# A three-block transformer kernel: the mixer's fourth query block moved ahead of the gate products, and bias rows spread from HBM to HBM

## The chip, the cores and the metric

The kernel runs on one core of a Trainium2 chip. A core has a matrix engine (TensorE, PE in the profile, with its weight loads as PEld), a vector engine (VectorE, DVE), an activation engine (ScalarE, ACT), a general-purpose engine (GpSimd, POOL) and SyncE (SP), which here only issues transfers. Each engine works through its own list of instructions in order and waits on semaphores for the others. Transfers run on 16 DMA engines. The metric is the device time of one execution in microseconds (us).

## The reference

The input x has 512 tokens of 1024 features, and all arithmetic is in float32. Two layers of a first kind are followed by one layer of a second kind:

```
for l in range(2):
    x = x + 0.5 * swiglu_ffn(x, ...)          # 1024 -> 2816 -> 1024
    h = rms_norm(x, mix_norm[l])
    x = x + hybrid_mixer(h, ...)
    x = x + 0.5 * swiglu_ffn(x, ...)
x = second_block(x, ...)                      # dilated attention + convolution, then an ffn
```

The hybrid mixer projects h with w_in and runs three attentions: a stick-breaking one (o_a), one over compressed, selected and window keys (o_b, "NSA", 8 heads), and one over indexed top keys (o_c, "DSA", 4 heads). Then it merges them with gates:

```
g_a, g_b, g_c = split(sigmoid(h @ w_gate), 3)
merged = g_a * (o_a @ w_br_a) + g_b * (o_b @ w_br_b) + g_c * (o_c @ w_br_c)
return merged @ w_out
```

The second block's attention adds a bias that depends on the distance of query and key: 8 rows (heads) of 384 numbers for each of three groups, each a table product of a 32 x 8 table with a 32 x 384 selection matrix plus a mask.

## The kernel before

**Numbers and weights.** A float32 product is made of three fast products: weights and activations are each split into a high and a low part (`split`, `w_prep`), and `mm3` (lines 172 to 174) issues high x high, high x low and low x high. Activations are kept with features on the partitions, so most products are 128 x 128 weights against 512 tokens. The weights come as one stream of 550 units of 128 x 1024 numbers (512 KB). A unit is loaded by SP into one of 3 staging buffers (`w_dma`, line 133), split by an ACT copy (line 141) and a DVE subtraction (line 142) into a ring of 5 slots, 3 units ahead of the products (`LOOK`), and used up by 24 matmuls.

**The first ffn.** `gen_ffn` makes 22 column groups; `up(cs)` takes 16 `mm3` for a group, and the first call takes groups 0 and 1 together and then makes the row norm (`stats_a`, `bcast`: DVE line 231, PE line 232), which the evacuation of every group needs. After `up` of group 2 in the very first ffn, `bias_rows` is called once: for each of three groups a small matmul (line 1015), a DVE addition into 8 rows of 384 numbers on partitions 0 to 7 (line 1018), and a POOL transfer (line 1019) that writes each row 128 times to the HBM buffer `dr_b` (3 x 8 x 128 x 384 numbers). `dr_b` is read in the second block only, on line 1172.

**The mixer.** There are two streams. The main stream, `gen_mix`, issues the projections, then 24 gate products (`tunit("w_gate", ...)`, evacuated on line 522 into the buffers at `M_IQ` and stored by POOL on line 523), then loads the first third of the gates again (line 530), and then forms the products with w_br_a (evacuated on line 538). All of these use the PSUM banks 0 and 1. The side stream, `gen_side`, does the attentions. `drive` interleaves them in the order in which instructions are written: it runs the side stream until it yields the name of a flag, and then steps the main stream until that flag is set. The order that results is only a priority: a planner that works with modelled times puts ready instructions of lower priority into the gaps. On the chip each engine's order is then fixed.

The NSA part, `gen_nsa`, has four query blocks b = 0 to 3 with n = 128 (b + 1) keys. A block has 8 calls of `attn_pair` (lines 760 to 803), each for two heads u: scores (PE line 777) into a bank of the first ring, addition of the mask with its maximum (DVE line 779), exponential (ACT line 781), scaling (DVE line 787), transposition (PE line 793) into a bank of the second ring, copy (ACT line 798), product with the values (PE line 801) into bank 7. A block opens with a matmul on line 898. The preparation of the next block (`prep`) is written into the middle of a block. The DSA part, `gen_dsa`, has four blocks of two such calls. `self.rings` names the two rings of banks, `self.p_ring` and `self.t_ring` the buffers for probabilities and their transposes. For b < 3 the rings are (2, 3, 4) and (5, 6). For block 3 it says:

```
if b == 3:
    yield "gates"
    self.rings = ((2, 3, 4), (5, 6, 0, 1))
...
self.p_ring = (p, p, p + [M_NQ], p + [M_NQ, M_IQ])[b][:4]
```

With n = 512, `p` has two buffers. The rings set for block 3 stay in force for the DSA part.

After both streams `gen_merge` forms the products with w_br_b and w_br_c over all 512 tokens, taking banks from a ring of all eight, adds them on DVE and POOL (lines 983 and 984), and multiplies with w_out.

Of the kernel before, what the change touches and what calls it, by code (L numbers as in the profile page):

```python
# [9 lines left out]
F32 = mybir.dt.float32  # L10
# [41 lines left out]
M_IQ = M  # L52
# [4 lines left out]
M_NQ = M_SV + 1024  # L57
# [52 lines left out]
class Build:  # L110
# [133 lines left out]
    def gen_ffn(self, wgu, wdn, l, done, halves=None):  # L244
        nc = self.nc
        Y = A_Y
        gs = [self.f(Y + 1536 + 512 * i, 512) for i in range(2)]
        tt = [self.f(Y + 2560 + 512 * i, 512) for i in range(2)]
        rb = self.f(A_RB, 512)
        ring = tuple(range(8))  # L250

        def fs(c):
            o = R_O + (c % FSLOTS) * 1024
            return self.r(o, 512), self.r(o + 512, 512)

        def gkey(c, up, k):
            return (wgu, l, np.arange(128 * k, 128 * k + 128), np.arange(128) + 128 * c + up * DFF)

        def evac(c, pg, pu):
            i = c % 2  # L260
            nc.vector.tensor_tensor(gs[i], pg, rb, op=ALU.mult)  # L261
            nc.scalar.activation(gs[i], gs[i], AF.Silu)
            nc.vector.tensor_tensor(gs[i], pu, gs[i], op=ALU.mult)  # L263
            hi, lo = fs(c)
            self.split(hi, lo, gs[i])

        def up(cs):
            ps = {(c, up): self.bank(ring) for c in cs for up in (0, 1)}
            order = [(c, up, k) for c in cs for up in (0, 1) for k in range(8)]
            if len(cs) == 2:  # L270
                order.sort(key=lambda e: e[2])
            for c, up, k in order:
                self.mm3(ps[c, up], self.w(gkey(c, up, k)), self.h(k), k == 0, k == 7)
                yield
            if len(cs) == 2:
                pst = self.bank(ring)
                self.bcast(self.stats_a((self.acc,), pst), tt_flat, pst, rb)
            for c in cs:
                evac(c, ps[c, 0], ps[c, 1])
            if cs[0] == 2 and self.first:  # L280
                self.first = False
                self.bias_rows()

        tt_flat = self.f(Y + 2560, 512)

        def down(grp, cs):
            nk = len(cs)
            if grp == 0:
                order = [(m, j) for m in range(8) for j in range(nk)]
            else:  # L290
                order = [(m, j) for m in range(2) for j in range(nk - 1)] + [(m, nk - 1) for m in range(2)]
                order += [(m, j) for m in range(2, 6 if halves else 8) for j in range(nk)]
            ps = {}
            for m, j in order:
                if j == 0:
                    ps[m] = self.bank(ring)
                key = (wdn, l, np.arange(128) + 128 * cs[j], np.arange(128) + 128 * m)
                self.mm3(ps[m], self.w(key), fs(cs[j]), j == 0, j == nk - 1)
                yield
                if j == nk - 1:  # L300
                    done(grp, m, ps[m], tt[m % 2], rb)
            if grp == 0 or not halves:
                return

            tl = {}
            for i in range(2):
                sl = slice(256 * i, 256 * i + 256)
                for m in (6, 7):
                    ps = self.bank(ring)[:, sl]
                    for j in range(nk):  # L310
                        if i == 0:
                            tl[m, j] = self.w((wdn, l, np.arange(128) + 128 * cs[j], np.arange(128) + 128 * m))
                        self.mm3(ps, tl[m, j], [a[:, sl] for a in fs(cs[j])], j == 0, j == nk - 1)
                        yield
                    done(grp, m, ps, tt[m % 2][:, sl], rb, sl)
                halves(i)

        c0 = list(range(11))
        c1 = list(range(11, 22))
        for cs in [(0, 1)] + [(c,) for c in range(2, 13)]:  # L320
            yield from up(cs)
        yield from down(0, c0)
        for c in c1[2:]:
            yield from up((c,))
        yield from down(1, c1)
# [516 lines left out]
    def gen_nsa(self, l):  # L842
        nc = self.nc
# [41 lines left out]
        nxt = prep(0)  # L885
        for b in range(4):
            q2, pts = nxt
            n = 128 * (b + 1)
            first = [None, None]
            if b == 3:  # L890
                yield "gates"
                self.rings = ((2, 3, 4), (5, 6, 0, 1))
            p = [M_P + 2 * n * i for i in range(1024 // n)]
            t = [o + 2 * n * i for i in range(512 // n) for o in (M_PT, M_SV)]
            self.p_ring = (p, p, p + [M_NQ], p + [M_NQ, M_IQ])[b][:4]
            self.t_ring = (t, t, t, t + [M_NQ + 1024])[b][:4]
            for g in range(2):
                first[g] = mm(ob[64 * g:64 * g + 64], lhsT=vc[:, 64 * g:64 * g + 64], rhs=pts, start=True, stop=True,
                              skip_group_check=True)
            for s in range(2):  # L900
                k = [[self.r(R_QK + 2048 * hl + 512 * (2 * s + g), 512) for hl in range(2)] for g in range(2)]
                for hh in range(4):
                    self.attn_pair([q2[:, 128 * (4 * g + hh):128 * (4 * g + hh) + 128] for g in range(2)], k,
                                   self.f(A_C + C_CM, 512)[:, 512 - n:512], n,
                                   gt[:, b, :, 1 + s].rearrange("p (g h) -> p h g", g=2)[:, hh],
                                   [V[:, :, s, g, :] for g in range(2)], ob[:, 128 * hh:128 * hh + 128], first)
                    self.bg(2)
                    if s == 1 and hh == 1:
                        nxt = prep(b + 1) if b < 3 else self.d_prep(0)
            o = self.r(R_O, 8192).rearrange("p (l c t) -> p l c t", l=2, c=8)[:, :, 2:6, 128 * b:128 * b + 128]  # L910
            self.split(o[:, 0], o[:, 1], ob.rearrange("p (c t) -> p c t", c=4))
# [27 lines left out]
    def gen_side(self, l):  # L939
        yield from self.gen_idx(l)  # L940
        yield from self.gen_cmp(l)
        yield "sb"
        self.sb_pair(0)
        yield "k"
        self.k_prep()
        self.k_tpose(0)
        yield "nq"
        self.q_prep(M_NQ, 8, 80, self.f(M_IQ + 1024, 128))
        self.sb_pair(1)
        self.k_tpose(1)  # L950
        yield "dq"
        self.q_prep(M_DQ, 4, 80 + 256, self.f(A_SM + 256, 64))
        self.rings = ((2, 3, 4), (5, 6))
        nxt = yield from self.gen_nsa(l)
        self.gen_dsa(l, nxt)


# [47 lines left out]
    def bias_rows(self):  # L1005

        nc = self.nc
        o = A_Y + 3584
        cb = self.f(o, 2304)[0:32]
        nc.scalar.dma_start(cb, self.ap["cb"])  # L1010
        tab = self.f(o + 2304, 24)[0:32]
        nc.scalar.dma_start(tab, self.ap["par"][2][0:32, 296:320])
        for g in range(3):
            ps = self.bank(tuple(range(8)))
            nc.tensor.matmul(ps[0:8, 0:384], lhsT=tab[:, 8 * g:8 * g + 8], rhs=cb[:, 384 * g:384 * g + 384],
                             start=True, stop=True)
            t = self.f(o + 2328 + 384 * g, 384)[0:8]
            nc.vector.tensor_tensor(t, ps[0:8, 0:384], cb[0:8, 1152 + 384 * g:1536 + 384 * g], op=ALU.add)
            nc.gpsimd.dma_start(self.dr_b[g], t[:, None, :].to_broadcast([8, 128, 384]))

    def gen_mix2(self):
        nc = self.nc
# [402 lines left out]
    def run(self, upto=99, start=0):  # L1425
        tc, nc, ap = self.tc, self.nc, self.ap
        with tc.tile_pool(name="sb", bufs=1) as sb, tc.tile_pool(name="hp", bufs=1) as self.hp, \
# [9 lines left out]
            self.sqt = [self.f(A_Y + 512 + 512 * i, 512) for i in range(2)]  # L1437
            self.dr_x = dr.tile([128, 4096], F32, name="dr_x")
            self.dr_b = dr.tile([3, 8, 128, 384], F32, name="dr_b")
            self.dr_c = dr.tile([8, 128, 512], F32, name="dr_c")  # L1440
            self.dr_s = dr.tile([512, 12], F32, name="dr_s")
            self.m2 = {}
# [17 lines left out]
            for l in range(2 if start == 0 else 0):  # L1460
                g = par[:, 24 * l:24 * l + 24]
                nxt = par[:, 24 * l + 24:24 * l + 32]
# [122 lines left out]
```

## Time and profile before

| what | value |
|---|---|
| time, median of 3 runs | 3531.94 us (3525.71 to 3532.26) |
| the profiled execution: its time | 3525.48 us |
| the profiled execution: its span, first to last instruction | 3523.7 us |
| mean granted clock of TensorE, as a share of full speed | 0.985 |
| PE busy | 3423.5 us (97%), 16884 records |
| DVE busy | 1998.7 us (57%) |
| ACT busy | 1316.1 us (37%) |
| POOL busy | 320.0 us (9%) |
| DMA traffic | 357.05 MB, mean 101 GB/s |

The busy time of PE is modelled from pipelined matmuls, so two stretches with the same busy share can hold different amounts of work; the number of matmul records in a stretch tells more. A matmul on plain float32 operands leaves two records. Where a line of the trace has "idle ... <-", what follows is the instruction that ended the wait. Times within the execution count from the start of the span.

### The profile page before, as it was taken

How to read it: one execution, taken by the hardware profiler on the slowest of the kernel's cores; microseconds unless marked ns; L12 is line 12 of the kernel's file. 1: busy time of each engine (PE TensorE's matmuls, PEld its weight loads, DVE VectorE, ACT ScalarE, POOL GpSimd, SP SyncE). 2: the span in 40 equal slices, each digit the busy share in tenths (PEclk: the TensorE clock that was granted, in tenths of full speed). 3: DMA queues.
4: the chain of work that ended last, by engine and by line, in shares of the span. 5: the costliest groups of instructions: out<-in, count | busy, mean ns of one | idle time of the engine just before them, and what ended most of it. 6: DMA issues, size and time to landing. Idle time of an engine off the chain costs nothing.

```text
span 3523.7 us, 43236 instructions
## 1 busy us (share of the span) xinstructions
PE 3423.5 (97%) x16884; PEld 2793.6 (79%) x16884; DVE 1998.7 (57%) x3733; ACT 1316.1 (37%) x2234; POOL 320.0 (9%) x355
## 2 busy tenths in 40 slices
PE   6899999999999999999999999999999999999997
PEld 5688888776888888888887768888877777878886
DVE  4344488566544444344886666443488998554344
ACT  3222354356332233223544464322344443443232
POOL 2000100010300010001000104000111112220002
PEclk8999999999999999999999999999999999999998
DMA  6722322331322222223322314223333224522221
GB/s 149 116 99 96 120 91 87 108 115 54 132 96 96 96 96 96 96 100 116 96 89 98 112 42 149 95 97 100 108 105 92 83 79 141 183 80 98 97 96 54
DMA packets 100814, 357.05 MB, mean 101 GB/s; under 512 B 14168, under 2 KB 16984, under 8 KB 99808
## 3 DMA queue, kind: packets, MB, share of 16 engines
q1 hardware_dynamic: 81504, 290.49, 24.6%
q0 software_dynamic: 18144, 61.76, 6.9%
q8 instruction: 132, 2.16, 0.3%
q10 hardware_dynamic: 960, 2.04, 0.2%
q14 instruction: 74, 0.61, 0.1%
HBM read 320.05 MB, written 32.08 MB: 100 GB/s over the span
## 4 chain that ended last, share of the span: by engine, by line
PE 91%; DMA 3%; DVE 3%; ACT 1%; issue 1%; POOL 0%; DVEq 0%; ACTq 0%; POOLq 0%
PE pb L172 27%; PE pb L173 27%; PE pb L174 27%; DMA af<-wst 2%; PE pb L801 2%; PE pb L793 1%; PE pb L777 1%; PE pb L1193 1%; PE pb L595 1%; PE pb L737 1%; PE pb L1290 1%; PE pb L1266 1%; PE pb L756 0%; DVE af L1351 0%; DVE ar L142 0%
## 5 line engine op out<-in xcount | busy, mean ns | idle before, releaser
L141 ACT ACTIVATE ar<-af 128x1024 fp32r<-128x1024 f32 x550 | 582.7, 1060 | 1517.5 <-PE pb L173 968.2
L172 PE MATMUL pb<-h,ar 128*128 128x512 f32 x2848 | 1114.2, 394 | 33.9 <-ACT ar L141 15.1
L174 PE MATMUL pb<-h,ar 128*128 128x512 f32 x2848 | 1120.1, 393 | 0.1
L173 PE MATMUL pb<-h,ar 128*128 128x512 f32 x2848 | 1119.4, 393 | 0.0
L142 DVE TENSOR_TENSOR ar<-af,ar 128x1024 fp32r<-128x1024 f32 x550 | 687.7, 1251 | 447.6 <-ACT ar L141 446.1
L172 PEld LDWEIGHTS pb<-h,ar 128*128 128x128 f32 x2848 | 538.0, 189 | 151.1 <-ACT h L239 16.2
L174 PEld LDWEIGHTS pb<-h,ar 128*128 128x128 f32 x2848 | 537.7, 189 | 114.6 <-issue 3.2
L173 PEld LDWEIGHTS pb<-h,ar 128*128 128x128 f32 x2848 | 537.9, 189 | 113.6 <-issue 3.2
L173 PE MATMUL pb<-ar 128*128 128x512 f32 (+1 forms) x1254 | 483.2, 386 | 1.2 <-DVE ar L183 1.2
L174 PE MATMUL pb<-ar 128*128 128x512 f32 (+1 forms) x1254 | 482.8, 386 | 0.0
L172 PE MATMUL pb<-ar 128*128 128x512 f32 (+1 forms) x1254 | 481.8, 386 | 0.6 <-DVE af L779 0.5
L172 PEld LDWEIGHTS pb<-ar 128*128 128x128 f32 x1254 | 235.6, 188 | 49.4 <-DVE af L779 1.2
L200 POOL TENSOR_TENSOR af<-af 128x512 f32<-128x512 f32 (+1 forms) x76 | 109.7, 1444 | 1816.5 <-ACT af L198 1805.5
L173 PEld LDWEIGHTS pb<-ar 128*128 128x128 f32 x1254 | 235.6, 188 | 49.0 <-DVE ar L183 2.4
L174 PEld LDWEIGHTS pb<-ar 128*128 128x128 f32 x1254 | 235.6, 188 | 47.1
L263 DVE TENSOR_TENSOR af<-pb,af 128x512 f32<-128x512 f32 x110 | 75.6, 690 | 299.0 <-PE pb L174 297.9
L261 DVE TENSOR_TENSOR af<-pb,af 128x512 f32<-128x512 f32 x110 | 75.5, 691 | 247.0 <-PE pb L174 231.9
L1132 DVE SCALAR_TENSOR_TENSOR af<-af 128x512 f32<-128x512 f32 x240 | 179.4, 748 | 3.6
L172 PE MATMUL pb<-ar,h 128*128 128x256 f32 (+1 forms) x448 | 133.4, 298 | 0.0
L173 PE MATMUL pb<-ar,h 128*128 128x256 f32 (+1 forms) x448 | 132.4, 296 | 0.0
L174 PE MATMUL pb<-ar,h 128*128 128x256 f32 (+1 forms) x448 | 132.0, 295 | 0.0
L180 DVE TENSOR_TENSOR ar<-af,ar 128x512 fp32r<-128x512 f32 (+4 forms) x178 | 114.3, 649 | 16.2 <-ACT ar L179 15.6
(236 smaller groups left out, 3185.3 us busy)
## 6 DMA issues: line engine op xcount, KB each, us to landing
af<-wst SPq DMA_DIRECT2D x550, 512.0 KB, 3.3
dr_g<-af POOLq DMA_DIRECT2D x64, 256.0 KB, 2.3
af<-dr_g POOLq DMA_DIRECT2D x24, 512.0 KB, 4.6
dr_x<-af POOLq DMA_DIRECT2D x3, 2048.0 KB, 7.5
af<-dr_x POOLq DMA_DIRECT2D x3, 2048.0 KB, 8.7
dr_b<-af POOLq DMA_DIRECT2D x3, 1536.0 KB, 63.3
h<-dr_g POOLq DMA_DIRECT2D x16, 256.0 KB, 5.5
af<-x POOLq DMA_DIRECT2D x8, 256.0 KB, 12.3
```

The lines of the kernel that those rows point to most:

```text
L141: self.nc.scalar.activation(self.r(o, UNIT), st, AF.Copy)
L142: self.nc.vector.tensor_tensor(self.r(o + UNIT, UNIT), st, self.r(o, UNIT), op=ALU.subtract)
L172: mm(out, lhsT=w[0], rhs=a[0], start=start, stop=False, skip_group_check=True)
L173: mm(out, lhsT=w[0], rhs=a[1], start=False, stop=False, skip_group_check=True)
L174: mm(out, lhsT=w[1], rhs=a[0], start=False, stop=stop, skip_group_check=True)
L180: self.nc.vector.tensor_tensor(lo, src, hi, op=ALU.subtract)
L200: nc.gpsimd.tensor_tensor(acc, acc, t, op=ALU.add)
L261: nc.vector.tensor_tensor(gs[i], pg, rb, op=ALU.mult)
L263: nc.vector.tensor_tensor(gs[i], pu, gs[i], op=ALU.mult)
L595: self.nc.tensor.transpose(ps[:, 128 * i:128 * i + 128], t[:, 128 * i:128 * i + 128], self.f(A_C + C_ID, 128))
L801: first[u] = self.behind(first[u], mm(out[64 * u:64 * u + 64], lhsT=v[u][:, j, :], rhs=pts[u][:, 128 * j:128 * j + 128], start=first[u] is ...
L1132: nc.vector.scalar_tensor_tensor(a, u[:, j:j + 512], w[:, j:j + 1], a, op0=ALU.mult, op1=ALU.add)
```

## The change

Three edits are made.

1. The NSA part no longer yields "gates" ahead of block 3, so block 3 and the DSA part are written, and so ranked, ahead of the gate products. As these hold the banks 0 and 1 and the buffers at `M_IQ`, block 3 and the DSA part keep the rings (2, 3, 4) and (5, 6), and the fourth probability buffer is dropped.
2. `bias_rows` is called after `up` of group 8 instead of group 2.
3. In `bias_rows`, the 8 rows go first to a small HBM buffer `dr_r`, and the 128-fold spreading reads from that buffer: a transfer from HBM to HBM.

```diff
-            if cs[0] == 2 and self.first:
+            if cs[0] == 8 and self.first:
                 self.first = False
                 self.bias_rows()
...
-            if b == 3:
-                yield "gates"
-                self.rings = ((2, 3, 4), (5, 6, 0, 1))
             p = [M_P + 2 * n * i for i in range(1024 // n)]
             t = [o + 2 * n * i for i in range(512 // n) for o in (M_PT, M_SV)]
-            self.p_ring = (p, p, p + [M_NQ], p + [M_NQ, M_IQ])[b][:4]
+            self.p_ring = (p, p, p + [M_NQ], p + [M_NQ])[b][:4]
...
-        nxt = yield from self.gen_nsa(l)
+        nxt = self.gen_nsa(l)
...
-            nc.gpsimd.dma_start(self.dr_b[g], t[:, None, :].to_broadcast([8, 128, 384]))
+            nc.gpsimd.dma_start(self.dr_r[g], t)
+            nc.gpsimd.dma_start(self.dr_b[g], self.dr_r[g][:, None, :].to_broadcast([8, 128, 384]))
...
+            self.dr_r = dr.tile([3, 8, 384], F32, name="dr_r")
```

## Rows read from the trace of the kernel before

**Rows 1.** The page: busy us (share of the span) and records of each engine.
```profile
PE 3423.5 (97%) x16884; PEld 2793.6 (79%) x16884; DVE 1998.7 (57%) x3733; ACT 1316.1 (37%) x2234; POOL 320.0 (9%) x355
```

**Rows 2.** The chain that ended last, in order of time: start us, us, what.
```profile
29.38 27.73 DMA af<-wst
...
87.50 47.47 DMA af<-wst
```

**Rows 3.** Windows of the start: stretch, us, busy us (records), PEclk, DMA share, GB/s.
```profile
40.00:70.00 30.00, 11.40 (x40) 8.28 (x39) 8.76 (x22) 6.54 (x7) 0.00 (x0) 0.66 0.45 106
110.00:150.00 40.00, 24.87 (x85) 18.52 (x84) 12.64 (x16) 10.55 (x14) 0.00 (x0) 0.79 0.89 138
40.00:50.00 10.00, 3.95 (x18) 2.94 (x16) 0.00 (x0) 0.00 (x0) 0.00 (x0) 0.82 0.49 76
110.00:120.00 10.00, 2.81 (x13) 1.99 (x11) 0.00 (x0) 0.00 (x0) 0.00 (x0) 0.91 0.99 93
220.00:260.00 40.00, 40.00 (x178) 33.15 (x177) 16.04 (x19) 8.49 (x8) 0.00 (x0) 1.00 0.29 96
```

**Rows 4.** POOL in order of time, 15 to 150 us: the three spreading transfers.
```profile
22.33 1.11 POOL L1019 DMA_DIRECT2D dr_b<-af  x1
...
74.27 1.09 POOL L1019 DMA_DIRECT2D dr_b<-af  x1 [47.80 <-DVE af L1018]
77.06 1.05 POOL L1019 DMA_DIRECT2D dr_b<-af  x1 [1.70 <-DVE af L1018]
```

**Rows 5.** DMA issues, 0 to 60 us: issues, KB each, us to landing.
```profile
dr_b<-af POOLq DMA_DIRECT2D x1, 1536.0 KB, 35.6
```

**Rows 6.** DMA issues of the whole page: issues, KB each, median us to landing.
```profile
af<-wst SPq DMA_DIRECT2D x550, 512.0 KB, 3.3
...
dr_x<-af POOLq DMA_DIRECT2D x3, 2048.0 KB, 7.5
...
dr_b<-af POOLq DMA_DIRECT2D x3, 1536.0 KB, 63.3
```

**Rows 7.** POOL's DMA queue, 30 to 57 us: packets, MB, share of 16 engines.
```profile
q0 software_dynamic: 280, 1.27, 43.8%
```

**Rows 8.** The same queue and the weight loads issued, 87 to 100 us.
```profile
q0 software_dynamic: 148, 0.68, 96.6%
...
af<-wst SPq DMA_DIRECT2D x2, 512.0 KB, 48.7
```

**Rows 9.** Windows of the two mixers, columns as in group 3.
```profile
800.00:870.00 70.00, 63.04 (x473) 45.84 (x473) 43.78 (x151) 44.92 (x111) 1.64 (x3) 1.00 0.05 15
...
2050.00:2120.00 70.00, 64.08 (x463) 46.70 (x463) 43.49 (x149) 44.45 (x110) 4.19 (x5) 0.93 0.08 24
```

**Rows 10.** DVE in order of time, first mixer: last gate product, last w_br_a product.
```profile
770.09 0.69 DVE L522 TENSOR_TENSOR af<-pb,af 128x512 f32<-128x512 f32 x1
...
791.98 0.69 DVE L538 SCALAR_TENSOR_TENSOR h<-h,pb 128x512 f32<-128x512 f32 x1
```

**Rows 11.** PE in order of time, first mixer: block 3's first scores.
```profile
800.65 1.17 PE L777 MATMUL pb<-ar 128*128 128x512 f32 x4
```

**Rows 12.** The same two moments in the second mixer, DVE and PE.
```profile
2042.61 0.69 DVE L538 SCALAR_TENSOR_TENSOR h<-h,pb 128x512 f32<-128x512 f32 x1 [0.69 <-PE pb L174]
...
2047.18 1.18 PE L777 MATMUL pb<-ar 128*128 128x512 f32 x4
```

**Rows 13.** Groups by line and shape, 800 to 870 us: busy us, mean ns.
```profile
L793 PE MATMUL pb<-af 128*128 128x128 f32 x116 | 17.5, 281 | 2.1 <-DVE af L787 1.1 <-DVE af L875 1.1
L781 ACT ACTIVATE af<-af 128x512 f32<-128x512 f32 x20 | 14.4, 719 | 4.9 <-DVE af L779 4.9
...
L798 ACT ACTIVATE af<-pb 128x512 f32<-128x512 f32 x22 | 12.6, 597 | 4.7 <-PE pb L793 4.7
...
L781 ACT ACTIVATION_READ_ACCUMULATOR af<-af 128x1 f32 x33 | 6.3, 190 | 0.0
```

**Rows 14.** Waits of PE, 800 to 870 us: us in total, times, longest.
```profile
PE pb L801 <- ACT af L798: 1.3, 3, 0.6
```

## The prediction

> **What bounds the kernel now.** I read the page first. PE is busy for 97% of the span [rows 1], so the work is bound by PE's own matmuls, and an edit that adds or removes none can only give back the stretches in which PE stands still or runs at its lower clock. The next view is the chain of waits in order of time. Outside PE it has two long pieces, both waits for a weight load, of 27.7 and 47.5 us [rows 2], where a load takes 3.3 us as a rule [rows 6]. So I looked at windows of the first 260 us. In steady work (220 to 260 us) PE leaves 178 records in 40 us, 4.45 per us [rows 3]. From 40 to 70 us there are 40 records, which is 40 / 4.45 = 9.0 us of work in 30; from 110 to 150 there are 85, which is 19.1 us of work in 40. The losses are 21.0 and 20.9 us, 41.9 together. [...]
>
> What the loads wait behind is seen in the DMA views. Just before each long load POOL issues the spreading transfers of the bias rows: one at 22.3 us, two at 74.3 and 77.1 [rows 4]. The first lands after 35.6 us [rows 5], the other two after 63.3 each [rows 6], where 63.3 is the median of the three and the first is the smaller. One alone keeps POOL's queue busy on 43.8% of the DMA engines' time, near half of them, and moves 1.27 MB in 27 us, 47 GB/s; two together take 96.6% and move 0.68 MB in 13 us, 52 GB/s [rows 7, 8]. Twice the engines move no more bytes. The two weight loads issued beside the pair take a median of 48.7 us [rows 8].
>
> Last I looked at the mixers, where the first edit acts. The end of the attention, 70 us in each mixer, is the one part where PE is not full: 63.0 and 64.1 us busy of 70 [rows 9].
>
> **The change part by part: the spreading transfer.** Its source moves from 8 partitions of SBUF to HBM; bytes, row length (384 numbers, 1536 bytes) and destination stay. What limits it now is common to one and to two transfers: not the number of engines, since the second set adds nothing, but the 8 source partitions or the writing into `dr_b`. HBM takes writes much faster from 128 partitions: 2048 KB in 7.5 us [rows 6]. So I take the source partitions as the limit, and the edit removes it. No row shows a transfer from HBM to HBM, so its cost is bounded from both sides. Fast end: 7.5 x 1536 / 2048 = 5.6 us on all engines, 11.3 us on half of them; of three transfers two share a half, 22.5 us for all. Slow end: no faster than now, 3 x 1.573 MB at the 49.7 GB/s of the pair (3.146 MB in 63.3 us) = 95 us. I take a value near the fast end, since the `dr_x` row is the nearest in what it does to HBM.
>
> [...]
>
> What a slow transfer costs depends on the weights in hand. The load issued at 87.5 us was late, and PE ran on until it had used 2.81 us of the window from 110, to 112.8: cover of 25.3 us [rows 2, 3]. At the first stall it was 29.4 to 43.95, only 14.6 us, the ring not having filled. The later place (after group 8 instead of 2) therefore matters too. A column group is 48 matmuls, at 4.45 per us 10.8 us, so with PE starting near 10 us group 8 ends near 107, and the three transfers are issued there, within some 10 us, when the ring is full. At the fast end a load waits 22.5 us at most, inside the cover, and the loss is nothing. Then both losses go: 41.9 us. I keep 3 us back for the ramp of the start and for loads that arrive late without stopping PE, and book -39.
>
> The added transfer to `dr_r` is three issues, which POOL must each see landed before the spreading issue. Behind it on POOL's queue stands nothing until the end of this ffn, hundreds of us later (POOL's view has no instruction after the third issue up to 150 us, [rows 4]), and SP's queue is not passed. `dr_b` is read far behind, in the second block. This costs nothing; without that cover it would be three short landings. The three small matmuls and additions only move.
>
> **The mixer.** Taking out the wait reorders the writing, so I asked what block 3 waits for now. In the first mixer the last gate product is evacuated at 770.1 us and the last w_br_a product at 792.0 [rows 10], and block 3's first scores start at 800.65 [rows 11]; in the second they are 2042.6 and 2047.2 [rows 12]. So block 3 starts 8.7 and 4.6 us after the last product of the main stream, when block 2 has got that far: the blocks before it, which stand ahead of the gates already, take so long that the gates are used up as filler first. The flag holds up nothing that was ready, and I book 0 gain.
>
> What remains of this edit is what it takes away: two of four banks for the transposed probabilities, and one of four probability buffers. A pair of heads in block 3 has two transpositions of four matmuls. A bank's turn is transposition, wait, copy (597 ns), and the copies share ACT with the exponentials (719 ns and 190 ns each) [rows 13]. Over 800 to 870 us ACT is 44.9 us busy and PE 63.0 [rows 9], so a bank has usually been copied when its turn comes, and PE's waits for a copy are 1.3 us now [rows 14]. Bounds: nothing, and one exponential with its read-out (0.9 us) for each of 16 pairs in a mixer (8 of block 3, 8 of DSA), 14.5 us per mixer. I take 1.5 us each, 3 together, nearer the low end as ACT has a third of that stretch free. In return the merge's first product (bank 0) may start before DSA ends in the first mixer; I leave that in the range.
>
> **Sum.** -39 + 3 = -36 us. Against the profiled execution's own 3525.5 us that is 3489.5. The median of the runs shown is 3531.9, 6.4 us above it, with one run at 3525.7; from the median it would be 3496. I put the forecast between, at 3493.
>
> **The rivals.**
>
> *A: part of the stall stays.* The copy from HBM reads the same 12 KB 128 times and runs at about half the fast end, 45 us for the three. Loads beside the pair now wait 48.7 of 63.3 us, 77%; 77% of 45 is 35 us, 10 beyond the cover, plus a restart at the lower clock: a loss of 10 to 20 us, 3503 to 3513. For it: no row excludes it. Against it: the writes at 7.5 us.
>
> *B, the other side: the copy is as slow as now, and the three now fall together.* 95 us in flight, 77% of it 73 us of wait, 48 beyond the cover and some clock: about 50 us lost in place of 41.9, and 3 in the mixer: 3525.5 + 11 = about 3537, or 3543 from the median. It decides once the three together run at no more than about 55 GB/s, today's rate. [...] Against it: the second half of the engines adds nothing today.
>
> *C: the gates do become filler.* If the new order leaves gate products for block 3 and DSA, PE's standing still there can fill: 7.0 + 5.9 = 12.9 us [rows 9], giving 3478 to 3482. For it: block 3 now ranks above the gates. Against it: blocks 0 to 2 rank above them already and still the gates end first. That this edit does nothing is part of my forecast.
>
> *D: the missing banks cost more,* 8 us or above in each mixer, toward the 14.5 bound: 3506 to 3519.
>
> **How the numbers follow.** Forecast (stall gone, mixer nearly unchanged) 0.64; A 0.14; B 0.07; C 0.10; D 0.05. The likeliest case runs from 3484 to 3502 with the two levels of the runs shown. For 8 in 10 I reach down into C and up through most of A and D: 3479 to 3514. Within 0.2% (7 us, about what a measurement of this kernel can tell from no change) lies little of any case: the edge of B and of a bad A, 0.05. Slower is the rest of B, 0.06; faster 0.89.
>
> **What would show it.** Right: no weight load above some 25 us to landing in the first 200 us; PE at 4.4 records per us and clock 1.00 from 40 to 150; the spreading copies landing in 10 to 25 us; in both mixers block 3's first scores the same distance behind the last gate product. Wrong: spreading copies of 40 us or more with a PE gap about 25 us behind their issue (A, B); gate products still running beside block 3 (C); PE waiting on line 798 copies before line 793 for many us (D).

## The result and the profile after

| | median us | lowest to highest | runs |
|---|---|---|---|
| before | 3531.96 | 3525.71 to 3532.26 | 4 |
| after | 3491.31 | 3489.11 to 3494.24 | 4 |

The ratio is 0.989, with a 95% interval from 0.9872 to 0.9907: the change makes the kernel faster by about 40 us, and the forecast was 3493. The profiled execution after took 3494.24 us, with a span of 3492.5 us and a mean granted clock of 0.988. Its page gives, for each engine, busy us, share of the span and records:

```profile
PE 3424.9 (98%) x16884; PEld 2795.8 (80%) x16884; DVE 2001.5 (57%) x3733; ACT 1320.5 (38%) x2236; POOL 320.4 (9%) x358
```

PE has the same 16884 records and nearly the same busy time as before [rows 1], so what was won is, in the main, time in which PE stood still. To see where, I use as marks the ACT copies on line 233, which end each row norm: one falls at the start of each mixer and one at its end.

| stretch between marks | before us | after us | difference |
|---|---|---|---|
| start of the span to the first mixer | 443.69 | 402.05 | -41.64 |
| first mixer | 530.46 | 532.76 | +2.30 |
| second mixer | 528.76 | 534.43 | +5.67 |
| both ffn between the mixers, second block, last ffn | 2020.8 | 2023.2 | +2.4 |

The sum, -31.2 us, is the difference of the two spans. The +2.4 of the last row lies behind the second mixer, where nothing was edited. The medians differ by more (40.7 us), since the profiled execution of before (3525.48 us) was shorter than the runs shown.

**The start.** Windows of the changed kernel, with the columns of [rows 3], first the start and then the two ends of the attention that answer to [rows 9]:

```profile
40.00:70.00 30.00, 30.00 (x132) 24.45 (x132) 15.81 (x20) 13.93 (x18) 0.00 (x0) 1.00 0.27 88
110.00:150.00 40.00, 40.00 (x175) 31.57 (x174) 17.18 (x21) 11.17 (x14) 4.87 (x6) 1.00 0.60 211
...
758.00:828.00 70.00, 64.94 (x457) 46.40 (x456) 45.35 (x152) 42.87 (x107) 0.00 (x0) 0.95 0.00 1
...
2011.00:2081.00 70.00, 63.90 (x439) 45.18 (x437) 44.53 (x150) 42.81 (x107) 1.32 (x3) 0.93 0.05 18
```

The 40 and 85 records of before [rows 3] are now 132 and 175, against 4.45 per us in steady work. Both stalls are gone, and with them the lower granted clock that followed each: it is 1.00 in both windows. In before it was 0.50 for 4 to 6 us behind each of PE's standstills there (18.6, 10.5 and 4.6 us), in the same columns:

```profile
62.55:66.55 4.00, 4.00 (x7) 2.49 (x8) 2.34 (x3) 0.60 (x1) 0.00 (x0) 0.50 0.38 131
123.30:128.10 4.80, 4.76 (x10) 3.31 (x11) 2.41 (x3) 0.47 (x1) 0.00 (x0) 0.50 1.00 98
136.18:141.80 5.62, 5.58 (x12) 3.96 (x13) 1.99 (x3) 1.74 (x3) 0.00 (x0) 0.50 0.84 269
```

The transfers of the page and of the first 200 us, with the number of issues, KB each and median us to landing:

```profile
af<-wst SPq DMA_DIRECT2D x550, 512.0 KB, 3.3
...
dr_b<-dr_r POOLq DMA_DIRECT2D x3, 1536.0 KB, 12.7
```

```profile
af<-wst SPq DMA_DIRECT2D x41, 512.0 KB, 3.3
...
dr_r<-af POOLq DMA_DIRECT2D x3, 12.0 KB, 2.8
```

A spreading copy lands in 12.7 us where it took 35.6 alone and 63.3 in a pair [rows 5, 6]. The 41 weight loads keep their median, and their longest is now 9.2 us (issued at 1.65 us; beside the copies it is 7.8), where the start of before had 49.9. POOL in order of time shows the new steps (start us, us, operation, and in brackets the idle time with what ended it):

```profile
113.44 0.54 POOL L1016 DMA_DIRECT2D dr_r<-af  x1 [87.71 <-DVE af L1015]
...
115.64 1.11 POOL L1017 DMA_DIRECT2D dr_b<-dr_r  x1
...
118.16 1.11 POOL L1017 DMA_DIRECT2D dr_b<-dr_r  x1 [0.90 <-DMA dr_r<-af]
128.99 1.08 POOL L1017 DMA_DIRECT2D dr_b<-dr_r  x1 [9.72 <-DMA dr_r<-af]
```

The third spreading issue waited 9.72 us for its 12 KB row transfer. That was issued at 116.76 us, behind one large copy in the same queue (issued at 115.64, landed at 128.33), and landed at 128.71, 11.95 us after its issue; of the other two row transfers one took 1.7 and one 2.8 us. The transfers issued from 116 to 128 us:

```profile
dr_r<-af POOLq DMA_DIRECT2D x1, 12.0 KB, 11.9
```

No other instruction of POOL was due then.

**The mixers.** DVE and PE in order of time, in the first and in the second mixer: the last w_br_a product of the main stream, and the first scores of block 3.

```profile
751.65 0.68 DVE L538 SCALAR_TENSOR_TENSOR h<-h,pb 128x512 f32<-128x512 f32 x1
...
2006.52 0.69 DVE L538 SCALAR_TENSOR_TENSOR h<-h,pb 128x512 f32<-128x512 f32 x1 [1.52 <-PE pb L174]
```

```profile
759.87 1.17 PE L777 MATMUL pb<-ar 128*128 128x512 f32 x4
...
2010.26 1.17 PE L777 MATMUL pb<-ar 128*128 128x512 f32 x4
```

Block 3 begins 8.2 and 3.7 us behind the main stream's last product; before it was 8.7 and 4.6 [rows 10 to 12]. The last gate product is evacuated (line 522) at 728.4 us, 31 us ahead of block 3. So the gates are no filler for block 3 in the new order either, and the wait that was taken out had held up nothing. In 70 us from about where block 3 opens PE has 457 and 439 records, 16 and 24 fewer than before [rows 9]; in windows that start as far from block 3's first scores as those of before it has 449 and 433.

### The profile page after: what moved, and what is told of

Same layout as the page of the kernel before. It is cut to its first block, busy times and chain, and to the rows that moved or that the text cites. A ratio compares the mean times of both kernels' runs of the same rounds, so it can differ in the third digit from the quotient of the medians.

```text
span 3492.5 us, 43251 instructions
## 1 busy us (share of the span) xinstructions
PE 3424.9 (98%) x16884; PEld 2795.8 (80%) x16884; DVE 2001.5 (57%) x3733; ACT 1320.5 (38%) x2236; POOL 320.4 (9%) x358
## 4 chain that ended last, share of the span: by engine, by line
PE 92%; issue 3%; DVE 3%; ACT 1%; DMA 1%; POOL 0%; DVEq 0%; POOLq 0%; ACTq 0%
PE pb L172 28%; PE pb L173 28%; PE pb L174 28%; PE pb L801 1%; PE pb L777 1%; PE pb L793 1%; PE pb L1191 1%; PE pb L1288 1%; PE pb L737 1%; PE pb L595 1%; PE pb L1264 1%; PE pb L756 0%; DVE af L1349 0%; DVE ar L142 0%; PE pb L751 0%
## 5 line engine op out<-in xcount | busy, mean ns | idle before, releaser
L172 PEld LDWEIGHTS pb<-ar 128*128 128x128 f32 x1254 | 235.5, 188 | 49.9 <-DVE h L538 0.9
## 6 DMA issues: line engine op xcount, KB each, us to landing
dr_b<-dr_r POOLq DMA_DIRECT2D x3, 1536.0 KB, 12.7
```

Of the source, the lines that this page charges most:

```text
L172: mm(out, lhsT=w[0], rhs=a[0], start=start, stop=False, skip_group_check=True)
```

## The experiments

Two theories stood against each other at each end. For the start: the transfer was slow because it read 8 partitions of SBUF (mine), or because one transfer keeps only near half of the engines busy (43.8% of their time [rows 7]), and the later place brought the gain. For the mixers: the missing banks and buffer cost some us (mine), or the new order itself costs or gives something. The last two columns of the table are the mixers by the marks.

| kernel | edit against before | median us | ratio (95%) | start | mixer 1 | mixer 2 |
|---|---|---|---|---|---|---|
| after | whole change | 3491.31 | 0.989 (0.9872 to 0.9907) | 402.05 | 532.76 | 534.43 |
| e1_bias_only | bias edits | 3483.79 | 0.9871 (0.9858 to 0.9885) | 402.25 | 530.43 | 528.58 |
| e2_mixer_only | mixer edit | 3533.19 | 1.0015 (1.0006 to 1.0024) | 443.95 | 530.48 | 531.28 |
| e3_place_only | later place | 3511.05 | 0.9947 (0.9933 to 0.9961) | 430.00 | 530.28 | 528.52 |
| e4_source_only | source in HBM | 3486.19 | 0.9878 (0.9865 to 0.9892) | 402.96 | 530.32 | 528.42 |
| e8_wide_source | 128 source partitions | 3490.91 | 0.9892 (0.9877 to 0.9907) | 404.88 | 532.62 | 532.11 |
| e5_banks_less | bias edits, 2 banks | 3491.32 | 0.9892 (0.9876 to 0.9909) | 402.63 | 531.05 | 535.11 |
| e6_buffer_less | bias edits, 3 buffers | 3485.43 | 0.9878 (0.9863 to 0.9892) | 401.73 | 531.12 | 528.44 |
| e7_both_less | bias edits, 2 banks, 3 buffers | 3492.49 | 0.9896 (0.9882 to 0.9911) | 401.84 | 529.42 | 536.93 |
| e12_three_banks | bias edits, 3 banks | 3490.88 | 0.9896 (0.9879 to 0.9912) | 401.40 | 528.33 | 536.35 |
| e10_whole_again | whole change | 3491.53 | 0.9899 (0.9884 to 0.9913) | 401.44 | 532.68 | 533.21 |
| e11_bias_again | bias edits | 3483.28 | 0.9874 (0.9859 to 0.9889) | 401.25 | 529.65 | 528.18 |
| e9_order_four_banks | bias edits, no wait, 4 banks | 3588.23 | 1.0171 (1.0151 to 1.0192) | 401.27 | 583.93 | 579.83 |

**The bias edits alone.** Mixer as before.

```diff
-            if cs[0] == 2 and self.first:
+            if cs[0] == 8 and self.first:
...
-            nc.gpsimd.dma_start(self.dr_b[g], t[:, None, :].to_broadcast([8, 128, 384]))
+            nc.gpsimd.dma_start(self.dr_r[g], t)
+            nc.gpsimd.dma_start(self.dr_b[g], self.dr_r[g][:, None, :].to_broadcast([8, 128, 384]))
```

> The later place and the HBM source of the bias rows alone; the mixer as before. The forecast's theory (both stalls of the start go, the mixer's edit gives nothing and costs a little): the start is as short as with the whole change, the two mixers as long as before, 530.5 and 528.8 us between the marks, and the time is 3 to 8 us below that of the whole change, 39 to 47 us below the kernel before. Rival, that the mixer's edit gave part of the gain: the time is above that of the whole change.

The whole gain of the start is there, and the kernel is 7.5 us faster than the whole change (3483.79 against 3491.31). The gain is the transfer's, and the mixer edit takes some of it back.

**The mixer edit alone.** The bias rows as before.

```diff
-            if b == 3:
-                yield "gates"
-                self.rings = ((2, 3, 4), (5, 6, 0, 1))
...
+            self.p_ring = (p, p, p + [M_NQ], p + [M_NQ])[b][:4]
...
+        nxt = self.gen_nsa(l)
```

> The mixer's edit alone (no wait for the gates, two banks and three buffers in block 3 and DSA); the bias rows as before. The forecast's theory: both stalls stay, and the time is 0 to 10 us above the kernel before; gate products still end before block 3 starts. Rival, that the wait held block 3 back: 5 to 15 us below the kernel before.

The ratio of 1.0015 is 5 us, from 2 to 8 by its interval: a loss by itself too, and no gain from the order. Its one profile is 6.7 us longer than that of before: 2.5 us in the second mixer, none in the first, and 3.9 behind the mixers, where nothing was edited.

**The later place alone.** Group 8, but the source stays in SBUF.

```diff
-            if cs[0] == 2 and self.first:
+            if cs[0] == 8 and self.first:
```

> Only the later place: the three spreading transfers still read 8 partitions of SBUF, after column group 8. The theory that the source partitions limit them: the three fall together and need 63 us or more, up to 95; the ring of weights covers about 25 us and PE stands still behind it, one long stall of 25 to 50 us in place of two; the time lies between 15 us below and 10 us above the kernel before. Rival, that the place alone gave the gain (a full ring covers the wait): 35 us or more below.

It won 13.7 of the 41.6 us of the start. Windows of this kernel behind the three issues, which POOL made from 113.6 us on, and its transfers from 0 to 240 us:

```profile
110.00:150.00 40.00, 40.00 (x174) 31.61 (x173) 10.84 (x14) 6.37 (x8) 3.25 (x3) 1.00 0.87 72
150.00:200.00 50.00, 34.00 (x131) 26.01 (x129) 8.51 (x10) 6.32 (x8) 0.00 (x0) 0.86 0.86 107
200.00:240.00 40.00, 35.52 (x145) 28.77 (x146) 21.55 (x25) 11.34 (x12) 0.00 (x0) 0.88 0.56 161
```

```profile
af<-wst SPq DMA_DIRECT2D x43, 512.0 KB, 4.3
...
dr_b<-af POOLq DMA_DIRECT2D x3, 1536.0 KB, 70.7
```

In the first of them the DMA engines count as busy for 87% of the time while 72 GB/s move; the longest landing is 101 us. PE runs on at full rate past 150 us on the weights in hand, and in the two windows behind it loses 92 and 33 records of the steady 223 and 178, about 28 us. It stands still three times, and the time is 15.7 us below before by the medians, just past the 15 that was given. PE in order of time, the end of the first standstill:

```profile
164.77 0.80 PE L172 MATMUL pb<-ar 128*128 128x512 f32 x1 [7.00 <-ACT ar L141]
```

So PE ran until 157.8 us. The load behind this standstill was issued at 121.9 us and landed 41.7 us later. The stall is put off and shortened, not removed.

**The source alone.** In HBM, at group 2 as before; the edit is the second half of that of the bias edits.

```diff
-            nc.gpsimd.dma_start(self.dr_b[g], t[:, None, :].to_broadcast([8, 128, 384]))
+            nc.gpsimd.dma_start(self.dr_r[g], t)
+            nc.gpsimd.dma_start(self.dr_b[g], self.dr_r[g][:, None, :].to_broadcast([8, 128, 384]))
```

> Only the HBM source, at the early place after column group 2, the first transfer near 22 us, when the ring of weights is not full and covers about 15 us. The theory that the source partitions limit the transfers: each lands within 10 to 15 us as with the whole change, and the time is 35 to 42 us below the kernel before, mixer as before. Rival, that the destination or the number of engines limits them, or that the place is needed: landings of 30 us and more, a stall near 45 us stays, and the time is 0 to 20 us below.

40.7 of the 41.6 us, at the early place. A window of this kernel where before stood still, and its transfer:

```profile
40.00:70.00 30.00, 30.00 (x128) 22.90 (x127) 17.08 (x29) 12.28 (x16) 2.12 (x3) 1.00 0.40 142
```

```profile
dr_b<-dr_r POOLq DMA_DIRECT2D x3, 1536.0 KB, 13.1
```

The copies landed after 16.2, 12.9 and 13.1 us. A weight load took 9.4 us at most in this kernel. With the source in HBM the place is worth 0.7 us of the start (402.96 against 402.25); the medians differ by 2.4, and their ranges touch (3483.98 to 3489.01 here, 3483.39 to 3484.67 with both).

**A wide source in SBUF.** To tell HBM from the number of partitions: each of the 8 rows is made on 16 partitions (the small product with a widened table, the mask added by a second product), and 128 partitions write 8 copies each, at group 2, mixer as before.

```diff
-            nc.gpsimd.dma_start(self.dr_b[g], t[:, None, :].to_broadcast([8, 128, 384]))
+            nc.gpsimd.dma_start(self.dr_b[g].rearrange("h (r j) n -> (h r) j n", j=8),
+                                t[:, None, :].to_broadcast([128, 8, 384]))
```

> As the kernel before (early place, source in SBUF, mixer untouched), but the small matmul writes each of the 8 rows to 16 partitions, the mask is added by a second matmul, and each of the 128 partitions is written 8 times to the same destination. The theory that few source partitions were the limit: each transfer lands within 6 to 15 us, no stall in the first 200 us, and the time is 35 to 43 us below the kernel before, as with the source in HBM. Rival, that SBUF as a source, or the repeated reading of it, is slow: landings of 30 us and more and a stall near 45 us.

The transfers of this kernel in its first 240 us:

```profile
dr_b<-af POOLq DMA_DIRECT2D x3, 1536.0 KB, 7.1
```

The same bytes into the same buffer from SBUF, in 7.1 instead of 35.6 to 63.3 us, and the stall is gone: neither SBUF as a source nor the writing was the limit. What is left is the 8 partitions, together with the pattern that began with them. By the medians the kernel is 4.7 us slower than with the HBM source; by the marks it loses 1.9 us in the start and 6.0 in the mixers. Nothing in the mixers was edited here. The planner lays the whole program out anew, and in the first mixer the order differs from that of before. In the second it does not: each engine runs the same instructions in the same order as in before, e1, e3, e4 and e11, which took 528.2 to 528.8 us there, and e8 took 532.1. This is its block 3's first scores and the mark at the end of its second mixer, 176.0 us apart:

```profile
2011.66 1.17 PE L777 MATMUL pb<-ar 128*128 128x512 f32 x4
...
2187.67 0.60 ACT L233 ACTIVATE af<-pb 128x512 f32<-128x512 f32 x1 [3.88 <-PE pb L232]
```

The order of the whole change, too, took 531.3 to 534.4 us in the second mixer (e2, e10, after). So one and the same order can differ by nearly 4 us in one mixer from one execution to another, and a price of 2 or 3 us in one mixer of one kernel is no finding by itself. The profiled execution of e8 is also the longest of its four (3493.62 us).

**Fewer banks, wait kept.** Block 3 keeps the flag "gates" and four probability buffers, but not the banks 0 and 1.

```diff
             if b == 3:
                 yield "gates"
-                self.rings = ((2, 3, 4), (5, 6, 0, 1))
```

> The bias rows as in the whole change, the wait for the gates kept, four probability buffers kept, but block 3 and DSA with two banks for transposes instead of four. Bias rows alone gave 3484 us, the whole change 3491. The theory that the loss of banks costs the 7 us: 3488 to 3492. Rival, that the order of writing costs it: 3483 to 3485.

**One buffer less, wait and four banks kept.**

```diff
-            self.p_ring = (p, p, p + [M_NQ], p + [M_NQ, M_IQ])[b][:4]
+            self.p_ring = (p, p, p + [M_NQ], p + [M_NQ])[b][:4]
```

> The bias rows as in the whole change, the wait and the four banks kept, but three probability buffers instead of four. The theory that banks cost the 7 us: no change against the bias rows alone, 3483 to 3485. Rival, that the buffer costs it: 3488 to 3492.

**Both less, wait kept:** the whole change but for the order; both diffs above together.

> The bias rows as in the whole change and the wait kept, with two banks and three buffers: all of the change but the order of writing. The theory that the wait held up nothing and the missing banks and buffer cost the 7 us: 3489 to 3493, as the whole change. Rival, that the order itself costs: 3483 to 3486. Second rival, that the order gains and the banks cost more than 7: 3495 or above.

The banks cost 7.5 us over the bias edits alone (3491.32 against 3483.79), the buffer 1.6, both 8.7. With both gone and the wait kept, the kernel stands at 3492.49, 1 us from the whole change: the order itself gives nothing and costs nothing that these runs can tell. By the marks the two kernels differ by 3 us in each mixer, in opposite directions.

**Three banks.**

```diff
-                self.rings = ((2, 3, 4), (5, 6, 0, 1))
+                self.rings = ((2, 3, 4), (5, 6, 0))
```

> The bias rows alone, but block 3 and DSA with three banks for transposes (5, 6, 0) instead of four; buffers and wait as before. If the banks cost by their number: between the bias rows alone and two banks, 3485 to 3489. If two are short and three enough: 3482 to 3486. If the planner's order decides and not the banks: anywhere from 3480 to 3495.

**The whole change and the bias edits again,** on one chip with the three banks.

> The whole change, beside the bias rows alone on the same chip. If the mixer's edit costs what the runs so far say: 6 to 9 us above the bias rows alone.

> The bias rows alone (later place and HBM source), mixer as before, beside the whole change on the same chip: 3482 to 3486 us, 6 to 9 below the whole change. If the difference seen before was one of chips: within 2 us of it.

3491.53 against 3483.28: 8.25 us, and no run of the one (3490.64 to 3494.24) reaches the other (3482.5 to 3484.19). Three banks cost as much as two (3490.88): the price isn't proportional to the banks taken, and of the three forecasts only the last, that the planner's order decides, contains this time. Where the price lies is seen by cutting the second mixer at block 3's first scores. With four banks, block 3 to the end of the mixer takes 172.9 to 173.8 us (before, e1, e3, e4, e11, all with one order), 171.5 with a buffer less, and 176.0 in e8; with two or three banks it takes 176.2 to 181.1 (after, e2, e5, e7, e10, e12). In the first mixer the same stretch shows no such price: 173.5 to 174.7 us with four banks, 172.2 to 175.6 with fewer. Windows of the first 60 us of that stretch in the second mixer, for the bias edits again, the whole change, both less, and last the buffer less:

```profile
2004.00:2034.00 30.00, 26.25 (x163) 17.68 (x162) 21.10 (x73) 18.01 (x44) 0.00 (x0) 0.89 0.01 5
2034.00:2064.00 30.00, 28.23 (x247) 21.79 (x246) 21.46 (x76) 22.62 (x62) 0.37 (x1) 1.00 0.01 1
```

```profile
2010.00:2040.00 30.00, 26.40 (x155) 16.91 (x156) 20.22 (x66) 16.82 (x40) 0.00 (x0) 0.83 0.04 16
2040.00:2070.00 30.00, 27.62 (x227) 20.53 (x223) 19.16 (x69) 20.86 (x56) 0.00 (x0) 1.00 0.01 2
```

```profile
2006.00:2036.00 30.00, 24.72 (x125) 15.45 (x126) 20.22 (x63) 15.04 (x37) 0.00 (x0) 0.72 0.06 18
2036.00:2066.00 30.00, 28.18 (x234) 20.99 (x229) 19.05 (x69) 20.39 (x54) 0.00 (x0) 1.00 0.01 1
```

```profile
2007.00:2037.00 30.00, 26.54 (x173) 18.58 (x173) 21.52 (x70) 17.53 (x43) 0.00 (x0) 0.83 0.00 1
2037.00:2067.00 30.00, 27.95 (x240) 21.27 (x239) 21.85 (x78) 22.17 (x62) 0.86 (x2) 1.00 0.06 19
```

410, 382 and 359 records in the 60 us, and 413 in the last kernel. At 247 records in 30 us, 8.2 per us, the second lacks 3.4 us and the third 6.2, most of what their last parts are longer (4.1 and 7.5 us). PE's busy time over the 60 us falls less (54.5, 54.0, 52.9 us), since records were longer at a lower granted clock (line 777: 456 ns at 0.89 and 531 at 0.72, below), and that is 0.83 and 0.72 in the first of the windows instead of 0.89. The clock alone does not explain the price, though: 0.06 and 0.17 of 30 us are an estimated 1.8 and 5.1 us, and the kernel with a buffer less has 0.83 as well and the shortest last part of all. Before and e8 have 0.83 there too, with four banks. Groups of the same kind in the first window, bias edits again and then both less (busy us, mean ns, idle before):

```profile
L777 PE MATMUL pb<-ar 128*128 128x512 f32 x32 | 10.9, 456 | 0.3 <-DVE af L779 0.3
...
L793 PE MATMUL pb<-af 128*128 128x128 f32 x40 | 6.3, 298 | 1.8 <-DVE af L787 1.1 <-ACT af L882 0.7
```

```profile
L777 PE MATMUL pb<-ar 128*128 128x512 f32 x26 | 11.0, 531 | 1.8 <-DVE af L779 1.8
L793 PE MATMUL pb<-af 128*128 128x128 f32 x32 | 6.8, 343 | 1.3 <-ACT af L882 0.7 <-ACT af L798 0.6
```

Of PE's waits in those 60 us of both less only 0.6 us is for a line 798 copy ahead of line 793, and the whole change has none; the form in which I had looked for the price is nearly absent.

What speaks for the banks: by the medians four kernels with four banks and an HBM source (e1, e4, e6, e11) took 3483.3 to 3486.2 us and five with fewer (after, e5, e7, e10, e12) 3490.9 to 3492.5, no run of the first reaches a run of the second, and the buffer and the wait were kept in some of the five and dropped in others. What keeps it from being shown: each choice of banks also has an order of its own from the planner, and e8, with four banks, has mixers as long as three banks have (1064.7 us for both). So the loss of 7 to 8 us goes with the banks, but whether by their number or by the order that the planner makes of them is open. That fewer transpositions are at hand to fill PE's gaps would fit, but was only argued.

**The new order with four banks.** No wait, but block 3 and DSA keep the banks 0 and 1. The main stream forms its sums in these banks too, and this kernel leaves out what kept the two apart, so sums of the mixers can be overwritten, and it doesn't compute the reference; which sums are hit was not traced. Its time is read only for where the work went.

```diff
             if b == 3:
-                yield "gates"
                 self.rings = ((2, 3, 4), (5, 6, 0, 1))
...
+            self.p_ring = (p, p, p + [M_NQ], p + [M_NQ])[b][:4]
...
+        nxt = self.gen_nsa(l)
```

> As the whole change, but block 3 and DSA keep the banks 0 and 1 as well, so the gate products, written later now, have to wait until DSA is through with them. The forecast's theory says that the gates, 24 x 24 matmuls at 4.45 per us or 129 us of PE in each mixer, are the filler of blocks 0 to 2: without them there PE stands still and they come at the end, 40 to 129 us more in each mixer, 80 to 260 in all. Rival, that the side stream is so much faster alone that little is lost: under 40 us in all.

Windows of the first mixer of this kernel, and POOL in order of time:

```profile
545.00:735.00 190.00, 163.42 (x980) 112.84 (x980) 125.29 (x449) 111.52 (x298) 0.00 (x0) 0.81 0.01 2
735.00:870.00 135.00, 135.00 (x606) 111.53 (x605) 47.64 (x51) 32.70 (x32) 18.93 (x35) 1.00 0.46 155
```

```profile
743.72 0.57 POOL L523 DMA_DIRECT2D dr_g<-af  x1 [222.26 <-DVE af L522]
```

The first gate is stored at 743.7 us. For 190 us the attention runs with hardly a weight loaded (2 GB/s) at a clock of 0.81 and with PE 163 us busy, and then the gates run alone. It costs 97 us against the whole change. This is about what the gates, and the products behind them, are worth as filler for the attention, and why the whole change takes the banks 0 and 1 from block 3.

## Why the prediction was right, point by point

**The stall goes: right, a little larger.** -39 was booked and -41.6 measured; the 3 us kept back for the ramp weren't needed. The signs named for it came: PE at 4.4 records per us and clock 1.00, copies in 12.7 us, no load above 9.2, and block 3's first scores 31.4 and 27.5 us behind the last gate product, where it was 30.6 and 27.5. So nothing of rival A, in which part of the stall stays, was seen. The cause was told rightly (8 source partitions): the HBM source and the wide SBUF source both remove it. The copy, 12.7 us at the median, is near the 11.3 us of the fast end on half the engines, 1.573 MB / 12.7 us = 124 GB/s; how many engines it used, no view shows. Both patterns begin with the dimension of 8, and with the source in HBM the copy was 2.8 to 5 times faster (12.7 against 35.6 and 63.3 us), so that dimension was not what limited it. From 8 partitions the rows give 44 GB/s for one transfer (1.573 MB in 35.6 us) and 50 for the pair; from 128 the same bytes took 7.1 us, 222 GB/s. Why 8 were slow is not shown, and no run changed the number of partitions alone: in e8 the pattern changed with it.

**The place: right in direction, of little weight.** I let it matter beside the source. With the source in HBM it is worth 0.7 us of the start (e4 against e1).

**Rival B, mis-sized.** It said that the slow copy at the later place would be slower than before, 3537 with 3 us for the mixer in it. The slow copy at that place, with the mixer as before (e3), ran at 3511, 16 us faster than before. The flight was about right (95 us said, 101 the longest landing), but I had let a load wait for 77% of the whole flight, 73 us; the longest landing of a load was 49.9 us, as before, and loads came through between: the one issued at 121.9 us landed at 163.6. About 28 us were lost where I had said 50. A full ring also covers more than I took. I had read 25.3 us, from a load issued at 87.5 us to PE's stop at 112.8; but that standstill ended with the load issued at 81.5 us (landed at 122.1), 31 us before the stop. In e3 PE stopped at 157.8 us, 36 us behind the issue of the load that it then lacked. The side "slower" was therefore not open in the way that I had described.

**The order gives nothing: right.** Block 3 stands as far behind the main stream as before, and e7 against e10 or after differs by about 1 us. Rival C did not happen.

**Banks and buffer: mis-sized.** +3 was booked, and 7.5 to 8.7 us measured (8.0 by the marks of the two profiles), of which the buffer is about 1.6 and the rest goes with the banks, most of it in the second mixer. I had taken 1.5 us a mixer between bounds of 0 and 14.5, on the ground that ACT was free a third of the time. That looks at how soon a bank is copied, and waits for a copy ahead of line 793 stayed at 0.6 us or none. What it leaves out is the rest of the order that the planner makes with fewer banks (28 and 51 records fewer in the 60 us of the second mixer) and the granted clock (0.83 and 0.72 instead of 0.89, an estimated 1.8 and 5.1 us); how much each adds stays open. The second mixer's +5.7 stays below the 8 us of rival D, and the first is far below.

**The sum.** -41.6 + 8.0 = -33.6 against -36, and +2.4 in stretches that the change doesn't touch. That 3493 met the median so closely is in part luck: the loss that I had set too low stands against the profiled execution of before, which was short for its kernel. By the profiled executions the time fell to 3494.2, 4.7 us above the sum's 3489.5; from the median the sum gave 3496, 4.7 above the measured one, and 3493 was set between.

**Faster than both.** The bias edits alone took 3483.3 to 3483.8 us, with ratios of 0.9874 and 0.9871: 43 and 45 us less than before on the same chips, and some 8 us less than the whole change.

## What to carry to other kernels

Before a small table is spread by a transfer, look at how many partitions it is read from: here a transfer from 8 partitions marked the DMA engines as busy (96.6% of their time for a pair), moved little (52 GB/s), and held up the loads of another queue (48.7 us at the median, against 3.3); a detour over HBM or a source on all partitions removed that (12.7 and 7.1 us to landing), and the place of the issue then mattered little (0.7 us). Before a wait is bought off with banks or buffers, look at whether the waiting side was ready earlier: here it was not, and the price was paid for nothing. Test the parts of a change apart: here a gain of 41 us hid a loss of 8. And before a few microseconds are put down to one part of it, look at how much the same order of instructions differs between executions: here nearly 4 us in one mixer.

## What the runs showed of the hardware that was not expected

- A transfer from HBM to HBM that reads each 1536-byte row 128 times moved 124 GB/s (1536 KB in 12.7 us), and the weight loads beside it took 7.8 to 9.4 us at most (after, e1, e4, e10).
- The slow transfers did not hold up loads for as long as they lasted: in e3, with the longest of three in flight for 101 us, no load took more than 49.9 us.
- A transfer of 12 KB landed after 11.95 us where one 1536 KB copy stood ahead of it in its queue, 0.4 us behind that copy; without one ahead it took 1.7 and 2.8 us. In e1 and e4 it is the same: 12.6 and 12.0 us, 0.4 and 0.2 us behind the copy, and 1.7 to 4.6 us without one ahead.
- The same instructions in the same order on every engine took 528.2 to 532.1 us in the second mixer of six kernels (before, e1, e3, e4, e8, e11). The granted clock over the 30 us behind block 3's opening was 0.89 in four of them and 0.83 in two (before, e8), but before took 528.8 us.
